# One ring of six PSUM banks for the front stage of a hybrid encoder layer

## The chip, the cores and the metric

The kernel runs on one core of a Trainium2 chip. The metric is the device time of one execution in microseconds (us); the kernel before takes 859.18 us, the median of three runs between 858.85 and 859.22. The engines are named as in the profile: PE (TensorE, matrix products), DVE (VectorE), ACT (ScalarE), POOL (GpSimd) and SP (SyncE, which only issues transfers here). PE writes its results into PSUM, which has eight banks; one bank holds a tile of 128 partitions by 512 numbers in fp32. A bank can be used again when the engines that read the result (DVE and ACT) are through with it.

## The reference

One layer of an encoder for a prompt and a sample, each of 256 tokens with 1024 features (512 tokens in all). From the normalised input one wide projection is made, cut into parts for three branches:

```
h = rmsnorm(x);  proj = h @ w_in          # 9952 columns
A: q,k,v = silu(conv5(...)); gated delta rule forward and backward, in chunks   (8 heads)
B: latent attention: q and k,v from low-rank latents, rotary key; softmax        (8 heads)
C: cross-attention into 256 memory tokens                                        (4 heads)
merged = sum over branches of sigmoid(gate) * ((branch * silu(z)) @ w_br)
y = rmsnorm(x + merged @ w_out) * final_gain
```

All is in fp32. Products whose precision matters are made from split operands, as described below.

## The kernel before, in words

**Products.** Features stand on the partitions and the 512 tokens along a row. `gemm` (L234) makes one tile of 128 output features by 512 tokens. Each operand is split into a rounded part `hi` (ACT, L210) and a rest `lo` (DVE, L214), and three products are summed (hi·hi, lo·hi, hi·lo), so a tile with 1024 input features takes 24 matmuls. `weight` (L199) loads a weight tile into one of two raw buffers and splits it into one of two `wh` and one of two `wl` buffers. `gemm_fm` is the same as `gemm`, done at once.

**Stages.** `run` (L1310) has a front (`front`, L1390), a middle and a back. The front makes the memory values (`mem_v`, L356), the memory keys, the four memory heads (`mem_attn`, L470), the latents, the decays, and two groups of four latent-attention heads (`mla_rope`, `mla_v`, `mla_qk`, `mla_attn`). Between these steps `fills` (L1374) takes products from a list: tiles of q, k and v for the delta rule (`qkv_tile`), merge gates (`gate_tile`) and others. From the first latent head on, the preparation of the delta rule (`gdn_prep`, L777) is drawn along in small pieces at a low priority. The middle runs the delta rule beside the rest of the fill list; there the order on PE is written out by hand (`weave`). The back makes the last branch and the output.

**One attention step** (`attend`, L298), for one head and one of the two sequences: score products into a bank `s_` (L308); maximum (DVE), exponentials with row sums (ACT, L322), scaling by the reciprocal sum (`p_`, L328 or L330); four transposes on PE into a bank `pt_` (L334), which are the turned probabilities; their split into `ph` (ACT) and `pl` (DVE) at L222 and L224; and six products with the values into a bank `oa` or `om` (L343), which one head keeps for both sequences. At the end of a latent head DVE multiplies this output into the gate `za` (L727); at the end of a memory head ACT copies it out (L486).

**PSUM before.** The front has a pool of eight banks under four tags; `self.banks` is 3:

- `gm`, three banks: all products of `gemm`, the fourth value tile (`vm3`, `v3`), some small sums
- `kk`, two banks: scores, the two rope products `ra` and `rb`, row sums (`ss_`) and broadcasts
- `ms0`, two banks: turned probabilities, value tiles 0 and 2, and of the delta-rule preparation `dp` of the forward direction (L807, two matmuls with a sum) and `kd` (L815, 128 small matmuls, read by DVE at L828, L856 and L858)
- `ms1`, one bank: attention outputs, value tile 1, `dp` of the backward direction

The middle and the back have a pool of their own over the same banks, with `self.banks` at 4: four `gm`, which also serve `kk`, two `ms0`, two `ms1`.

**What sets the order.** In the front the order of every engine's instructions is made by a planner of the framework when the kernel is built. It goes by the order in the source, shifted by the stated `high_priority` offsets (a latent head's attention stands 50 instructions earlier, weight splits 60, weight loads 1000, the preparation 300 later), and issues on each engine the first instruction that its model of the times takes to be ready. A tile counts as ready to be written when a bank of its tag is free in that model. On the chip each engine then runs its instructions in that fixed order, and waits where a result or a bank is late. The weights' transfers are issued on SP's queue, the copies to DRAM on ACT's and SP's. `issue_after` puts instructions behind a named one on the same engine. In the middle, PE's order is fixed by `weave` and doesn't depend on the planner.

Of the kernel before, what the change touches and what calls it, by code (L numbers as in the profile page):

```python
# [7 lines left out]
F32 = mybir.dt.float32  # L8
# [5 lines left out]
P = 128  # L14
# [142 lines left out]
class Layer:  # L157
# [9 lines left out]
        return self.ps.tile([P, 512], F32, tag="gm", bufs=self.banks, name=name)  # L167

    def ps_kk(self, name):
        if self.banks == 4:  # L170
            return self.ps_gm(name)
        return self.ps.tile([P, 512], F32, tag="kk", bufs=2, name=name)

    def ps_ms(self, par, name):
        return self.ps.tile([P, 512], F32, tag=f"ms{par}", bufs=1 if par and self.banks == 3 else 2, name=name)

    def big(self, i, name, dt=F32R):

# [177 lines left out]
    def mem_v(self):  # L356
        nc, A = self.nc, self.A
        ms = []
        warm = self.p0.tile([P, 1], F32, name="warm")
        nc.vector.memset(warm, 0.0)  # L360
        nc.scalar.activation(warm, warm, AF.Square)

        zero = self.s2("zero", F32R)
        nc.vector.memset(zero.bitcast(F32), 0.0)
        zp = self.ps_kk("zp")
        for i in range(10):
            nc.tensor.matmul(zp, zero[:, 0:P], zero, start=i == 0, stop=i == 9)

        vps = [self.ps_gm(f"vm{tb}") if tb == 3 else self.ps_ms(tb % 2, f"vm{tb}") for tb in range(4)]
        acc = self.s2("mem2")  # L370
        raws = []
        with self.tc.high_priority(offset=1000):
            for k in range(8):
                if k % 2 == 0:
                    pair = self.big(k // 2, f"memT{k}", F32)
                raw = pair[:, k % 2]
                wr = self.pa.tile([P, 512], F32, tag="V", bufs=8, name=f"wr_vm{k}")
                nc.sync.dma_start(raw, A["memT"][:, k])
                d = (nc.sync if k else nc.scalar).dma_start(
                    wr, A["wvm"][k // 2][:, (k % 2) * 512:(k % 2 + 1) * 512])  # L380
                if k == 0:
                    nc.sync.dma_start(self.prm, A["prm"])
                raws.append((raw, wr))
        self.after = d.ins
        for k, (raw, wr) in enumerate(raws):
            hl = self.pk.tile([P, 2, 512], F32R, tag="kq", bufs=8, name=f"mh{k}")
            hi = self.p0.tile([P, 1024], F32R, tag="wh", bufs=2, name=f"wh_vm{k}")
            lo = self.p0.tile([P, 1024], F32R, tag="wl", bufs=2, name=f"wl_vm{k}")
            if k:
                nc.scalar.activation(hi[:, :512], wr, AF.Copy)  # L390
            else:
                nc.vector.tensor_scalar(hi[:, :512], wr, 1.0, None, ALU.mult)
            rnd = self.split(raw, hl[:, 0], hl[:, 1], self.mg[:, k:k + 1])
            nc.vector.tensor_tensor(lo[:, :512], wr, hi[:, :512].bitcast(F32), op=ALU.subtract)
            ms.append((hl[:, 0], hl[:, 1]))
            for i, (a, b) in enumerate(((0, hi), (1, hi), (0, lo))):
                for tb in range(4):
                    t = slice(tb * P, (tb + 1) * P)
                    nc.tensor.matmul(vps[tb], ms[k][a][:, t], b[:, :512],  # L399
                                     start=k == 0 and i == 0, stop=k == 7 and i == 2)  # L400
            with self.tc.issue_after(rnd.ins) if k == 0 else nullcontext():
                self.add_square(acc, raw, k, 1)
        self.mem_xs = ms
        self.cst = self.p0.tile([P, _CST.shape[1]], F32, name="cst")
        nc.sync.dma_start(self.cst, A["cst"])
        rm = self.rms_cols(acc, "mem")
        self.vm = []
        for tb in range(4):
            hi = self.pa.tile([P, 512], F32R, tag="V", bufs=8, name=f"vmh{tb}")
            lo = self.pa.tile([P, 512], F32R, tag="V", bufs=8, name=f"vml{tb}")  # L410
            self.split(vps[tb], hi, lo, rm[:, tb:tb + 1])
            self.vm.append((hi, lo))
        self.rm = rm
# [261 lines left out]
    def mla_v(self, g):  # L675

        nc, A = self.nc, self.A
        hi, lo = self.weight(A["wv"][g], 1024, f"wv{g}")
        vt = self.vt = []
        for tb in range(4):  # L680
            if tb == 2:
                self.fills(1)
            t = slice(tb * P, (tb + 1) * P)
            ps = self.ps_gm(f"v{g}{tb}") if tb == 3 else self.ps_ms(tb % 2, f"v{g}{tb}")
            n = 0
            for a, j in ((hi, 0), (hi, 1), (lo, 0)):
                for k in range(2):
                    nc.tensor.matmul(ps, self.kl[k][j][:, t], a[:, k * 512:(k + 1) * 512],
                                     start=n == 0, stop=n == 5)
                    n += 1  # L690
            vh = self.pa.tile([P, 512], F32R, tag="V", bufs=8, name=f"vh{g}{tb}")
            vl = self.pa.tile([P, 512], F32R, tag="V", bufs=8, name=f"vl{g}{tb}")
            self.split(ps, vh, vl)
            vt.append((vh, vl))
# [615 lines left out]
    def run(self):  # L1310
        nc = self.nc
        with ExitStack() as st:

            stp = ExitStack()
            self.ps, self.banks = self.pool(stp, "ps", bass.MemoryType.PSUM, reuse_waits="tile"), 3
            dp = self.pool(st, "dr", bass.MemoryType.DRAM)
            self.d_v = dp.tile([8, 512, P], F32, name="d_v")
            self.d_r = dp.tile([2, 32, 2, 384], F32, name="d_r")
            self.d_om = dp.tile([P, 4, 512], F32, name="d_om")
            self.d_z = dp.tile([P, 8, 512], F32, name="d_z")  # L1320
            self.d_xm = dp.tile([P, 4, 512], F32, name="d_xm")
            self.d_xa = dp.tile([P, 8, 512], F32, name="d_xa")
            self.d_n = dp.tile([8, 512], F32, name="d_n")
            self.d_m = dp.tile([8, P, 512], F32, name="d_m")
            self.d_g = dp.tile([2, 8, P, 512], F32, name="d_g")
            self.plan()
            self.p0 = self.pool(st, "p0")
            sth, stx = ExitStack(), st.enter_context(ExitStack())
            self.sth, self.stx = sth, stx
            self.ph = self.pool(sth, "ph", side="right")  # L1330
            self.setup()
            self.pk = self.pool(st, "pk")
            self.pb = self.pool(st, "pb")
            with ExitStack() as st2:
                self.pa = self.pool(st2, "pa")
                self.front()
            stp.close()
            self.ps, self.banks = self.pool(st, "pq", bass.MemoryType.PSUM, reuse_waits="tile"), 4
            with ExitStack() as st2:
                self.pg = self.pool(st2, "pg")  # L1340
                self.middle()
            with ExitStack() as st2:
                self.pe = self.pool(st2, "pe")
                self.back()
# [270 lines left out]
```

## Time and profile before

| | before |
|---|---|
| median of three runs | 859.18 us |
| the profiled execution | 859.05 us |
| its span, first to last instruction | 857.3 us |
| instructions | 13230 |
| PE busy | 845.6 us (99%), 4822 matmuls |
| DVE busy | 573.4 us (67%) |
| ACT busy | 451.9 us (53%) |
| POOL busy | 145.4 us (17%) |
| granted PE clock, mean | 0.999 |
| front / middle / back, by PE's products | to 369 us / 369 to 761 us / from 761 us |

A row of the timeline has the start in us from the span's start, the duration, the engine, the line of the kernel, the operation, the tiles it writes and reads, the shapes, and how many like it were merged; in brackets stands how long the engine was idle before it and what ended that. Matmuls overlap in the pipeline, so their durations are longer than the time that each adds; the spacing of their starts is what counts. A row in the list of waits has the engine and what it was about to do, what it waited for, the total in us, how often, and the longest. A row of the table of windows has, for PE, PEld (weight loads), DVE, ACT and POOL, the busy time and the count, then the granted clock, the share of the transfer engines and GB/s.

### The profile page before, as it was taken

To read this page: it belongs to the slowest core of one execution; us is meant where nothing else is said; L and a number is where in the kernel's file an instruction comes from. 1 tells how busy PE (TensorE), PEld (TensorE's weight loads), DVE (VectorE), ACT (ScalarE), POOL (GpSimd) and SP (SyncE) were. 2 spreads that over 40 slices of the span, in tenths; PEclk is the share of its full clock that TensorE was granted. 3 is DMA by queue.
4 is the path that set the end of the run, shared out by engine and by line. 5 is a ranking of instruction groups with operands and counts; after the bars stand their busy time and mean duration, and the time that the engine had idled before them with its cause. 6 is when DMAs were issued, how large, how long until landed. Compare 5 with 4: busy or idle time off the path is not lost.

```text
span 857.3 us, 13230 instructions
## 1 busy us (share of the span) xinstructions
PE 845.6 (99%) x4822; PEld 698.4 (81%) x4822; DVE 573.4 (67%) x1021; ACT 451.9 (53%) x891; POOL 145.4 (17%) x135
## 2 busy tenths in 40 slices
PE   9999999999999999999999999999999999999997
PEld 7878888888888888878788888888888888888886
DVE  7776347687599998457689998684555544346543
ACT  7655455455474465546775748666663632223232
POOL 0200111000100002072101254213110002332121
PEclk9999999999999999999999999999999999999999
DMA  9422222442425525363334365546445447375332
GB/s 326 141 79 87 86 81 68 139 138 75 103 77 164 137 90 146 116 191 129 109 103 122 117 189 174 152 134 180 132 122 160 138 134 250 118 241 160 116 98 99
DMA packets 68273, 116.10 MB, mean 135 GB/s; under 512 B 24048, under 2 KB 31600, under 8 KB 68208
## 3 DMA queue, kind: packets, MB, share of 16 engines
q1 hardware_dynamic: 46560, 104.51, 38.6%
q10 hardware_dynamic: 21648, 10.75, 4.6%
q8 instruction: 38, 0.62, 0.3%
q14 instruction: 27, 0.22, 0.1%
HBM read 95.09 MB, written 16.99 MB: 131 GB/s over the span
## 4 chain that ended last, share of the span: by engine, by line
PE 95%; DVE 2%; ACT 1%; issue 1%; DMA 1%; POOL 0%; POOLq 0%; ACTq 0%; DVEq 0%; SPq 0%
PE gm_qkv L246 16%; PE gm_g L246 16%; PE gm_z L246 8%; PE gm_bm L246 5%; PE gm_bg L246 5%; PE gm_za L246 5%; PE y L1256 5%; PE vm L399 3%; PE gm_be L246 3%; PE gm_qm L246 3%; PE gm_km L246 3%; PE kk L971 3%; PE o L1121 2%; PE gm_qn L246 2%; PE gm_cq L246 2%; PE s_a L308 2%
## 5 line engine op out<-in xcount | busy, mean ns | idle before, releaser
L745 DVE SCALAR_TENSOR_TENSOR kq<-cz,prm,kq 128x510 f32<-128x510 f32 (+1 forms) x64 | 48.1, 752 | 6.0 <-ACT kq L738 5.0
L246 PE MATMUL gm_qkv<-hh,wh_qkv 128*128 128x512 f32 x192 | 51.1, 400 | 0.5 <-ACT wh_qkv L210 0.5
L246 PE MATMUL gm_g<-hl,wh_g 128*128 128x512 f32 x192 | 51.5, 399 | 0.0
L246 PE MATMUL gm_g<-hh,wl_g 128*128 128x512 f32 x192 | 51.3, 398 | 0.0
L246 PE MATMUL gm_g<-hh,wh_g 128*128 128x512 f32 x192 | 51.1, 401 | 0.1
L246 PE MATMUL gm_qkv<-hh,wl_qkv 128*128 128x512 f32 x192 | 50.3, 397 | 0.0
L246 PE MATMUL gm_qkv<-hl,wh_qkv 128*128 128x512 f32 x192 | 49.7, 396 | 0.0
L214 DVE TENSOR_TENSOR wl_qkv<-wr_qkv,wh_qkv 128x1024 fp32r<-128x1024 f32 x24 | 31.1, 1297 | 25.9 <-ACT wh_qkv L210 10.1
L214 DVE TENSOR_TENSOR wl_g<-wr_g,wh_g 128x1024 fp32r<-128x1024 f32 x24 | 30.1, 1254 | 22.0 <-PE gm_g L246 11.7
L246 PEld LDWEIGHTS gm_qkv<-hl,wh_qkv 128*128 128x128 f32 x192 | 35.8, 188 | 8.2
L246 PEld LDWEIGHTS gm_qkv<-hh,wh_qkv 128*128 128x128 f32 x192 | 35.3, 188 | 8.9 <-ACT wh_qkv L210 1.2
L246 PEld LDWEIGHTS gm_qkv<-hh,wl_qkv 128*128 128x128 f32 x192 | 35.5, 188 | 7.8
L246 PEld LDWEIGHTS gm_g<-hl,wh_g 128*128 128x128 f32 x192 | 35.4, 188 | 7.7
L246 PEld LDWEIGHTS gm_g<-hh,wl_g 128*128 128x128 f32 x192 | 35.3, 188 | 7.5
L246 PEld LDWEIGHTS gm_g<-hh,wh_g 128*128 128x128 f32 x192 | 35.1, 188 | 7.8 <-ACT wh_g L210 0.3
L210 ACT ACTIVATE wh_qkv<-wr_qkv 128x1024 fp32r<-128x1024 f32 x24 | 25.4, 1058 | 29.1 <-PE gm_qkv L246 8.6
L1256 PE MATMUL y<-wh_wo,mh 128*128 128x512 f32 (+1 forms) x144 | 39.9, 370 | 0.0
L210 ACT ACTIVATE wh_g<-wr_g 128x1024 fp32r<-128x1024 f32 x24 | 25.4, 1060 | 26.0 <-PE gm_g L246 11.6
L961 POOL TENSOR_TENSOR kl<-kq,kh 128x512 fp32r<-128x512 f32 x16 | 22.8, 1427 | 94.8 <-ACT kh L959 94.8
L1226 POOL TENSOR_TENSOR mg<-mg,lg 128x512 f32<-128x512 f32 x16 | 27.2, 1700 | 59.0 <-DVE lg L1225 59.0
L246 PE MATMUL gm_bm<-xa,wh_bm 128*128 128x512 f32 x128 | 33.5, 398 | 0.0
L246 PE MATMUL gm_bg<-xg,wh_bg 128*128 128x512 f32 x128 | 32.5, 395 | 0.0
(432 smaller groups left out, 2199.5 us busy)
## 6 DMA issues: line engine op xcount, KB each, us to landing
wr_g<-in_w_dram SPq DMA_DIRECT2D x24, 512.0 KB
wr_qkv<-in_w_dram SPq DMA_DIRECT2D x24, 512.0 KB
e<-d_r SPq DMA_DIRECT2D x64, 96.0 KB
wr_z<-in_w_dram SPq DMA_DIRECT2D x12, 512.0 KB
d_g<-gt_g ACTq DMA_DIRECT2D x16, 256.0 KB
wr_za<-in_w_dram SPq DMA_DIRECT2D x8, 512.0 KB
wr_bm<-in_w_dram SPq DMA_DIRECT2D x8, 512.0 KB
lg<-d_g SPq DMA_DIRECT2D x16, 256.0 KB
```

Of the source, the lines that this page charges most:

```text
L210: self.wround = nc.scalar.activation(hi[:, :n], raw[:, :n], AF.Copy).ins
L214: d = eng.tensor_tensor(lo[:, :n], raw[:, :n], hi[:, :n].bitcast(F32), op=ALU.subtract)
L246: nc.tensor.matmul(ps[:m], a[:, k * m:(k + 1) * m], xs[k][j], start=n == 0, stop=n == 3 * nk - 1)
L308: nc.tensor.matmul(sp[:, qb * 256:(qb + 1) * 256], a, b, start=j == 0, stop=j == n - 1)
L399: nc.tensor.matmul(vps[tb], ms[k][a][:, t], b[:, :512], start=k == 0 and i == 0, stop=k == 7 and i == 2)
L745: nc.vector.scalar_tensor_tensor(ys, zs, self.cw[:, f, m:m + 1], ys, ALU.mult, ALU.add)
L961: nc.gpsimd.tensor_tensor(lo, src, hi.bitcast(F32), op=ALU.subtract)
L971: nc.tensor.matmul(ps, a[:, k], b, start=i == 0, stop=i == 2)
L1121: nc.tensor.matmul(out, ub[:, d, s, cp], rhs, start=n == 0, stop=n == 3)
L1226: nc.gpsimd.tensor_tensor(self.merged[d], self.merged[d], gt, op=ALU.add)
L1256: nc.tensor.matmul(ps, xs[2 * j + q][a][:, t], b[:, q * 512 + c0:q * 512 + c1], start=j == 0 and n == 0, stop=j == 3 and n == 5)
```

## The change

`self.banks` is 6 in the front: `gm` has six banks and serves products, scores, rope products, row sums and broadcasts, and whatever had `ms0` (turned probabilities, value tiles 0 and 2, `dp` forward, `kd`). `ms1` has two banks: attention outputs, value tiles 1 and 3, `dp` backward. So the shared part is six banks in place of 3 + 2 + 2, and the outputs have two in place of one. The pool of the middle and the back, with four banks in `gm` and two each in `ms0` and `ms1`, is as it was.

```diff
     def ps_gm(self, name):
         return self.ps.tile([P, 512], F32, tag="gm", bufs=self.banks, name=name)

     def ps_kk(self, name):
-        if self.banks == 4:
-            return self.ps_gm(name)
-        return self.ps.tile([P, 512], F32, tag="kk", bufs=2, name=name)
+        return self.ps_gm(name)

-    def ps_ms(self, par, name):
-        return self.ps.tile([P, 512], F32, tag=f"ms{par}", bufs=1 if par and self.banks == 3 else 2, name=name)
+    def ps_ms(self, par, name):
+        if self.banks == 6 and not par:
+            return self.ps_gm(name)
+        return self.ps.tile([P, 512], F32, tag=f"ms{par}", bufs=2, name=name)
...
-        vps = [self.ps_gm(f"vm{tb}") if tb == 3 else self.ps_ms(tb % 2, f"vm{tb}") for tb in range(4)]
+        vps = [self.ps_ms(tb % 2, f"vm{tb}") for tb in range(4)]
...
-            ps = self.ps_gm(f"v{g}{tb}") if tb == 3 else self.ps_ms(tb % 2, f"v{g}{tb}")
+            ps = self.ps_ms(tb % 2, f"v{g}{tb}")
...
-            self.ps, self.banks = self.pool(stp, "ps", bass.MemoryType.PSUM, reuse_waits="tile"), 3
+            self.ps, self.banks = self.pool(stp, "ps", bass.MemoryType.PSUM, reuse_waits="tile"), 6
```

## The prediction

> **What bounds the kernel now.** I read the page's shares and slices first, then a table of windows, then the list of what TensorE (PE) waited for, and last the timeline around each of those waits.
>
> ```profile
> PE 845.6 (99%) x4822; PEld 698.4 (81%) x4822; DVE 573.4 (67%) x1021; ACT 451.9 (53%) x891; POOL 145.4 (17%) x135
> ...
> PE   9999999999999999999999999999999999999997
> ...
> PEclk9999999999999999999999999999999999999999
> ```
>
> PE is busy from end to end at the full clock. A busy PE is not yet a PE at its peak, so the windows and the spacing come next: the two windows are the front from 120 us on and the middle.
>
> ```profile
> 120.00:369.00 249.00, 245.85 (x1377) 205.56 (x1377) 191.00 (x371) 136.73 (x271) 13.97 (x13) 1.00 0.38 113
> 369.00:760.00 391.00, 391.00 (x2484) 322.68 (x2483) 256.49 (x468) 214.97 (x456) 99.51 (x92) 1.00 0.48 148
> ```
>
> The middle has no idle PE at all; the front leaves 249.00 - 245.85 = 3.15 us. The chain of waits gives the spacing of matmuls that nothing holds up:
>
> ```profile
> 144.12 0.44 PE pt_m L334 x4
> ...
> 362.76 0.60 PE oa L343 x5
> ...
> 375.02 5.58 PE gm_g L246 x24
> ```
>
> So one matmul of 512 columns takes 5.58 / 24 = 0.2325 us of PE, one of 256 columns 0.60 / 5 = 0.12, one transpose 0.44 / 4 = 0.11. The amount of matmul work is the same after the change, so it can win only what lies between these spacings. PE's waits:
>
> ```profile
> PE oa L343 <- DVE za L727: 1.1, 1, 1.1
> ...
> PE pt_a L334 <- ACT p_a L328: 0.6, 1, 0.6
> PE gm_qkv L246 <- ACT wh_qkv L210: 0.5, 1, 0.5
> PE s_m L308 <- ACT p_m L322: 0.4, 1, 0.4
> PE oa L343 <- DVE pl_a L224: 0.4, 1, 0.4
> ```
>
> Each occurs once. The first and the fourth are waits for a PSUM bank; the second and the fifth wait for data; the third waits for a rounded weight.
>
> **The change part by part.** No instruction is added or removed. What changes is which bank a result may use, and through that the order in which the planner lays out all engines, their DMA issues included.
>
> *Scores from the ring of six.* A score tile had two banks, and this one waited until the exponentials (ACT) had read the bank before last:
>
> ```profile
> 135.68 0.28 PE L308 MATMUL s_m<-km,qml 128*128 128x256 f32 x1
> ...
> 135.79 0.47 ACT L322 ACTIVATE p_m<-s_m,nb_m 128x256 f32<-128x256 f32 x1
> ...
> 136.40 0.50 PE L308 MATMUL s_m<-km,qmh 128*128 128x256 f32 x2 [0.45 <-ACT p_m L322]
> ```
>
> The next matmul was due at 135.68 + 0.12 = 135.80 and came at 136.40: 0.60 us lost, removed by a free third bank. Nothing else is due there in its place.
>
> *Two banks for attention outputs.* `oa` had one bank, which the next head could not write before DVE had multiplied it into `za`:
>
> ```profile
> 251.90 0.60 PE L334 MATMUL pt_a<-cst,p_a 128*128 128x128 f32 x4
> ...
> 252.89 0.69 DVE L727 TENSOR_TENSOR za<-za,oa 128x512 f32<-128x512 f32 x1
> ...
> 253.63 0.39 PE L343 MATMUL oa<-ph_a,vh 128*128 128x256 f32 x1 [1.13 <-DVE za L727]
> ...
> 255.17 0.86 PE L246 MATMUL ra<-qlh,wh_ra 128*128 128x512 f32 x3
> ...
> 257.27 0.60 PE L334 MATMUL pt_a<-cst,p_a 128*128 128x128 f32 x4
> ...
> 257.94 1.24 PEld L246 LDWEIGHTS gm_g<-hh,wh_g 128*128 128x128 f32 x6 [0.31 <-ACT wh_g L210]
> ```
>
> Due at 251.90 + 0.44 = 252.34, come at 253.63: 1.29 us. The rope product `ra` is also given a bank of the six; it could stand only behind the scores' two banks before and came at 255.17. Earlier, it would cover this hole and free its rounded-weight buffer sooner for `wh_g`, for which PE waited at 257.94 (due at 257.27 + 0.44 = 257.71, so 0.23 us). These two go together: 1.52 us.
>
> *Turned probabilities and the sums (`dp`, `kd`) from the six.* This is where the order changes most.
>
> ```profile
> 216.14 0.40 PE L809 MATMUL dp<-dr00tb,bd 128*128 128x512 f32 x1
> ...
> 216.46 1.30 PE L823 MATMUL kd<-kq 128*32 128x32 f32 x128
> ...
> 219.34 0.91 ACT L328 ACTIVATE p_a<-p_a,rs_a 128x256 f32<-128x256 f32 x2 [0.75 <-DVE rs_a L325]
> ...
> 234.87 0.40 PE L809 MATMUL dp<-dr00ct,bd 128*128 128x512 f32 x1
> ...
> 240.46 0.60 PE L334 MATMUL pt_a<-cst,p_a 128*128 128x128 f32 x4
> ...
> 241.67 0.68 DVE L858 TENSOR_TENSOR nd<-nd,kd 128x512 f32<-128x512 f32 x1
> ```
>
> `dp` (half summed at 216.14, finished at 234.87) and `kd` (216.46, last read at 241.67) sat in both banks that turned probabilities may use. The probabilities were ready at 219.34 + 0.91 = 220.25 and were turned only at 240.46: attention stood still for 20 us. PE lost nothing meanwhile, since fill products covered it, but the backlog then ran in one bunch up to 257, and the hole at 252 lies in that bunch. From six banks the turn can follow at once; its own worth is nothing (cover: the fills) and its effect is in the 1.52. If attention goes first, the delta-rule preparation on DVE goes later. It has room, since its next reader on POOL waits for the front's last `oa` anyway, whose buffers it reuses:
>
> ```profile
> POOL t L893 <- PE oa L343: 27.1, 1, 27.1
> ```
>
> 27 us of delay would cost nothing there.
> The Trainium skill, in Perfetto Trace Analysis, section Optimization Strategy, says that the same gap repeated on the engine that should be saturated can mean too little SBUF or PSUM for the next tile; by that rule PSUM is not short here, because no PE gap repeats, and the sum would be 859.05 unchanged, while the rows above show a shortage that makes no gap where it lies.
>
> *Values (`vm`, `v`) two in the six, two in the output pair; row sums and broadcasts from the six.* Nothing: no such tile is in the list of waits. Without cover, as much as the scores' wait, 0.60 each way.
>
> *What stays.* The wait for a rounded weight:
>
> ```profile
> 170.72 0.63 PE L246 MATMUL gm_kn<-klh,wl_kn 128*128 128x512 f32 x2
> ...
> 171.86 2.12 PE L246 MATMUL gm_qkv<-hh,wh_qkv 128*128 128x512 f32 x8 [0.51 <-ACT wh_qkv L210]
> ```
>
> Due at 170.72 + 2 x 0.2325 = 171.19, come at 171.86: 0.67 us, no bank in it. And the drain of the last head, behind which the middle's PE order begins:
>
> ```profile
> 363.20 1.80 PE L246 MATMUL gm_za<-hh,wl_za 128*128 128x512 f32 x7
> ...
> 365.19 0.88 PE L334 MATMUL pt_a<-cst,p_a 128*128 128x128 f32 x4
> 366.62 0.55 PE L334 MATMUL pt_a<-cst,p_a 128*128 128x128 f32 x3 [0.55 <-ACT p_a L328]
> 367.11 0.38 PE L343 MATMUL oa<-ph_a,vh 128*128 128x256 f32 x1
> 367.86 0.38 PE L343 MATMUL oa<-pl_a,vh 128*128 128x256 f32 x1 [0.37 <-DVE pl_a L224]
> ...
> 369.28 1.09 PE L246 MATMUL gm_qkv<-hh,wh_qkv 128*128 128x512 f32 x4
> ```
>
> 366.62 - (365.19 + 0.44) = 0.99, then 0.16 before 367.11 and 0.63 before 367.86: 1.8 us, on ACT and DVE, not on banks. The middle's new pool lies on the same banks; before, its first product followed the last `oa` by 0.12, so it waited for none. At worst it waits for one reader, 0.7 (the DVE multiplication by `oa`).
>
> *What the new order brings in.* The trace of before cannot show it. Every PE wait is one that the planner did not foresee, and a new order has its own. Lower bound: it also rids itself of the rounded-weight wait and the drain, -0.67 - 1.8 = -2.5. Upper bound: three waits as dear as the dearest row, 3 x 1.29 = +3.9. I take one wait of the size of the `wh_qkv` row, +0.5, as that is the commonest size in the list.
>
> **Sum.** -0.60 - 1.52 + 0.5 = -1.6. From the profiled execution's 859.05 this is 857.4. The median shown is 859.18, 0.13 above; I leave that out.
>
> **The rivals.**
>
> *Waits only change place* (859.0). Attention is a chain through DVE and ACT, and in the window from 120 to 369 DVE is busy 191 of 249 us. Where a bank no longer holds a step, the DVE behind it may: the hole at 252.34 needs `pl`, which DVE also makes. For it: the two data waits in the list, 1.0 us. Against it: six `oa` matmuls of the waiting head and nine of `ra` could have gone at 252.34.
>
> *The drain and the weight wait go too* (854.9). 859.05 - 2.12 - 0.67 - 1.8 = 854.5, and 0.4 for a wait as small as the `pl_a` row. For it: scores of the last head no longer need the bank of the head before. Against it: the drain's own rows wait for ACT and DVE.
>
> *Slower: fills are spent too early* (862.6). With more banks to draw from, the planner runs products ahead, and the last heads of both groups of four (246 to 258, and 360 to 369) stand without products beside them. The price of a bare chain is in the drain: the last za matmuls before it start at 363.20, and from there to the first `oa` of that head, 367.11, and its second, 367.86, are 3.9 to 4.7 us. Two bare chains cost up to 2 x 4.7 = 9.4 in place of the 1.29 + 0.23 + 1.8 = 3.3 there now, +6.1; with a part of it covered as today, half to two thirds, +3.5. It decides as soon as the last product of a group of heads ends before the last scores begin. Against it: attention is traced with a priority 50 instructions earlier, and the products it needs come out in the same order as before.
>
> *Long tenants crowd the six* lies inside that rival's price: `dp` and `kd` hold two of the six for 20 to 25 us, and four remain where products and scores had five.
>
> *The clock falls.* The first products of the program show what a lower clock would cost:
>
> ```profile
> L367 PE MATMUL zp<-zero x10: 396/632/796, 1.5 to 5.4; 128*128 128x512 f32 x10
> ```
>
> Ten starts in 3.9 us are 0.43 each, 0.2 more than 0.2325; a stretch of twenty at that pace costs 4 us: 861.4 with the gains kept. For it stands nothing in the rows from 17 us on, whose clock is 1.00.
> The Trainium skill, in TensorE: Matmul & The Clock Gate, section A second HAM failure mode: psum-queue depth-cycling, tells of a kernel whose cycling through PSUM banks left PE idle so often for moments that its clock went up and down; here the granted clock was 0.999 with the smaller rings, and no run yet shows the larger one.
>
> *The change does nothing* is part of the first rival: the planner would lay out the same order, which the 20 us stand-still makes unlikely.
>
> **How the numbers follow.** Forecast 857.4, chance 0.42, own range 856.4 to 858.4. Waits change place 0.23. Drain and weight wait go too 0.15. Fills spent too early 0.18. Clock 0.02. A measurement of this kernel tells about 0.2% from no change, 1.7 us: faster is under 857.46, slower over 860.9. The forecast's own spread lies across the lower bound; I count 0.27 of its 0.42 as faster. Faster: 0.27 + 0.15 = 0.42. Same: 0.15 + 0.23 and a little of the slower case, 0.39. Slower: 0.17 + 0.02 = 0.19. The range leaves out the far half of the slower case and a third of the best: 855.0 to 861.6.
>
> **What would show it.** Right: no wait of `oa` for `za` and none of scores for `p_m` in the list; `pt_a` within about 5 us of its probabilities after 216 us; the first `oa` to the last in a narrower bunch before the group's end; the middle's first product 1 to 2 us earlier than 369.28, and everything behind it moved by the same. Wrong: new PE waits of together over 2 us in the front; a drain before the middle's first product over 3 us; a middle that is no longer full, or a clock under 0.99.

## The result and the profile after

The changed kernel takes 958.19 us (median of 4 runs, 956.5 to 959.14) against 859.16 before: 1.1149 times as long, interval 1.1136 to 1.1162. The forecast was 857.4, the range ended at 861.6. It is 99 us slower, and the profiled execution (958.18 us, span 956.4) is read below.

The page's shares and slices of the kernel after:

```profile
span 956.4 us, 13220 instructions
...
PE 885.7 (93%) x4822; PEld 723.0 (76%) x4822; DVE 578.7 (61%) x1021; ACT 454.1 (47%) x891; POOL 143.6 (15%) x135
...
PE   9988687899977899988899999999999999999997
...
PEclk9997787999989899989899999999999999999999
```

PE has the same 4822 matmuls and is idle for 7% in place of 1%. Both the holes and the lower clock lie in the first half of the slices. The table of windows, with columns for PE, PEld, DVE, ACT and POOL and then the granted clock, says where:

```profile
0.00:120.00 120.00, 101.96 (x441) 81.76 (x442) 69.93 (x111) 59.50 (x102) 9.48 (x12) 0.89 0.36 124
120.00:369.00 249.00, 215.40 (x1087) 174.73 (x1086) 155.50 (x309) 103.91 (x194) 11.62 (x9) 0.92 0.27 82
369.00:470.00 101.00, 88.37 (x413) 71.21 (x412) 49.34 (x81) 46.00 (x94) 11.59 (x13) 0.92 0.38 115
470.00:860.00 390.00, 390.00 (x2478) 321.85 (x2477) 256.08 (x467) 215.32 (x457) 89.85 (x84) 1.00 0.46 143
```

The middle is as full as before (390.00 of 390.00 at clock 1.00). The front is not, and it ends later:

```profile
467.21 0.41 PE L343 MATMUL oa<-ph_a,vl 128*128 128x256 f32 x1
467.43 1.05 PE L246 MATMUL gm_qkv<-hh,wh_qkv 128*128 128x512 f32 x2
```

The middle's first product starts at 467.43 in place of 369.28: 98.15 of the 99 us. PE's list of waits (total, times, longest):

```profile
PE pt_a L334 <- ACT p_a L328: 18.2, 14, 3.3
PE pt_m L334 <- DVE p_m L330: 15.1, 4, 6.9
PE oa L343 <- ACT ph_a L222: 6.3, 9, 0.9
PE oa L343 <- DVE pl_a L224: 5.6, 7, 1.7
PE ss_q L267 <- POOL cqs L260: 4.1, 1, 4.1
PE rp L598 <- DVE ga L593: 3.3, 2, 2.9
PE om L343 <- ACT ph_m L222: 2.7, 4, 0.7
PE ss_k L267 <- POOL cks L260: 2.6, 1, 2.6
```

No row here waits for a bank. PE waits for data: turned probabilities (`pt`) for the softmax, outputs (`oa`, `om`) for the split of the turned tile, the sums (`ss`, `rp`) for POOL and DVE. One memory head shows it in the timeline of PE:

```profile
112.56 0.41 PE L308 MATMUL s_m<-km,qml 128*128 128x256 f32 x1
115.67 0.48 PE L334 MATMUL pt_m<-cst,p_m 128*128 128x128 f32 x1 [2.69 <-DVE p_m L330]
...
118.75 0.58 PE L343 MATMUL om<-ph_m,vmh 128*128 128x256 f32 x1 [0.69 <-ACT ph_m L222]
...
120.71 0.41 PE L334 MATMUL pt_m<-cst,p_m 128*128 128x128 f32 x1
120.78 2.06 PE L246 MATMUL gm_qm<-hh,wh_qm 128*128 128x512 f32 x4
122.63 1.91 PE L246 MATMUL gm_qm<-hl,wh_qm 128*128 128x512 f32 x4
```

After the last score product of the head's first sequence PE does nothing until the probabilities are there, and then begins to turn them. The products of the next head (`gm_qm`) come only at 120.78, right behind the first transpose of the second sequence (120.71), though nothing that they read is missing: both parts of their weights were ready at 101.3. And they run slowly: four from 120.78 to 122.63 are 0.46 us each, against 0.2325 before.

To size the two losses I went through the starts of successive PE matmuls, from the first of `vm` to the last of `oa`. What a distance has above 0.232, 0.118 or 0.108 us (512, 256, 128 columns) is booked as a wait if PE was idle in between, as slow running if it was not idle and the distance is over half as long again. Some 2.5 us of the slow running are very short products that every kernel has, and drop out of a difference. The rest of the front is 353 to 355 us of work in these two kernels.

```
front, us       length   waits   slow running
before          362.75     4.5       4.4
after           460.9     74.4      32.1
```

So 69.9 us of the 98.15 are waits and 27.7 slow running; 0.5 is left over.

**Where the order comes from.** In both kernels the first writers of all tiles of one tag stand on PE strictly in the order in which the program creates them; tiles of different tags pass each other. Before, 70 of 146 tiles of the front begin on PE after one that was created later, always one of another tag; after, 18. PE's instructions as the planner laid them out, around the first memory head:

```
before: s_m00, s_m01, abp, gm_qm1 x24, gm_cq0 x16, pt_m00 x4, gm_cq x12, pt_m01 x4, ... om0
after:  abp, s_m00 x6, pt_m00 x1, s_m01 x6, pt_m00 x3, om0 x6, pt_m01 x1, gm_qm1 x16, pt_m01 x3
```

Before, 40 products lie between scores and turn, which cover the softmax. After, a turned tile and the products draw on one ring. A bank of that ring goes to tiles in order of creation, so the products of the next head, created later, can't begin before the first transpose, which waits for the softmax. Counted in instructions at full speed, PE had 3.6 to 33.8 us of other work between the scores and the first transpose of an attention step before; after, 0 to 2.3 us in 20 of the 24 steps. This I call theory A. Its rivals: B, too many tenants in too few banks; and C, the clock falling by itself, because more banks are cycled through.

### The profile page after: what moved, and what is told of

Same layout as the page of the kernel before. It is cut to its first block, busy times and chain, and to the rows that moved or that the text cites. A ratio compares the mean times of both kernels' runs of the same rounds, so it can differ in the third digit from the quotient of the medians.

```text
span 956.4 us, 13220 instructions
## 1 busy us (share of the span) xinstructions
PE 885.7 (93%) x4822; PEld 723.0 (76%) x4822; DVE 578.7 (61%) x1021; ACT 454.1 (47%) x891; POOL 143.6 (15%) x135
## 4 chain that ended last, share of the span: by engine, by line
PE 87%; ACT 5%; DVE 5%; issue 2%; POOL 1%; DMA 0%; ACTq 0%; POOLq 0%; DVEq 0%; SPq 0%
PE gm_qkv L246 14%; PE gm_g L246 14%; PE gm_z L246 7%; PE gm_bm L246 5%; PE gm_bg L246 5%; PE y L1256 4%; PE gm_za L246 4%; PE gm_qm L246 3%; PE vm L399 2%; PE gm_be L246 2%; PE gm_km L246 2%; PE kk L971 2%; PE o L1121 2%; PE s_a L308 2%; PE gm_cq L246 2%
## 5 line engine op out<-in xcount | busy, mean ns | idle before, releaser
L246 PE MATMUL gm_qkv<-hh,wh_qkv 128*128 128x512 f32 x192 | 54.5, 422 | 0.0
L214 DVE TENSOR_TENSOR wl_g<-wr_g,wh_g 128x1024 fp32r<-128x1024 f32 x24 | 30.6, 1277 | 30.8 <-ACT wh_g L210 15.7
L246 PEld LDWEIGHTS gm_qkv<-hh,wh_qkv 128*128 128x128 f32 x192 | 38.2, 205 | 8.4
L214 DVE TENSOR_TENSOR wl_qkv<-wr_qkv,wh_qkv 128x1024 fp32r<-128x1024 f32 x24 | 31.0, 1294 | 16.6 <-ACT wh_qkv L210 8.1
L224 DVE TENSOR_TENSOR pl_a<-pt_a,ph_a 128x512 fp32r<-128x512 f32 x16 | 11.0, 687 | 42.4 <-ACT ph_a L222 42.1
```

The source lines that it names most:

```text
L214: d = eng.tensor_tensor(lo[:, :n], raw[:, :n], hi[:, :n].bitcast(F32), op=ALU.subtract)
L224: nc.vector.tensor_tensor(lo, src, hi.bitcast(F32), op=ALU.subtract)
L246: nc.tensor.matmul(ps[:m], a[:, k * m:(k + 1) * m], xs[k][j], start=n == 0, stop=n == 3 * nk - 1)
```

## The experiments

**One extra instruction (theory A against B).** The tile takes its bank with a product that needs no probabilities; the first transpose then overwrites it. The ring stays at six.

```diff
         tp = self.ps_ms(0, "pt_" + name)
+        nc.tensor.transpose(tp[:, 0:P], self.c("id"), self.c("id"))
```

> The kernel after with one transpose of the constant identity put ahead of the four transposes of each turned-probability tile: 24 short instructions more, written into the same bank and overwritten; ring, tags and source order as after. Theory A (banks of one tag are granted in source order, so a turned-probability tile that waits for its softmax holds back every product traced behind it): the tile's bank is claimed without waiting for the softmax, products go ahead, time 857 to 863 (before, plus 24 x 0.11 = 2.6, minus up to 2.1 of old waits), no PE wait of a transpose for p above 1.5 us in one piece except at the end of the front, granted clock 0.99 or more. Theory B (six banks are too few for all tenants): each bank is held through the softmax too, some 5 us longer, so at least as slow as after, 958 or more. Theory C (the clock falls because results cycle through more banks, and the waits follow from that): the same banks are cycled, clock at most 0.96, 945 or more.

881.17 us, 1.0253 of before (1.0237 to 1.0268), 18 us above the range given for theory A and far below those of B and C; front 384.95, waits 17.5, slow running 11.8. One more transpose per step takes back 77 of 99 us with the ring unchanged, so it is the place of the first writer that cost them. PE's waits in this kernel:

```profile
PE ss_q L267 <- POOL cqs L260: 4.1, 1, 4.1
PE rp L599 <- DVE ga L594: 2.9, 1, 2.9
PE ss_k L267 <- POOL cks L260: 2.6, 1, 2.6
PE rkb L282 <- POOL rk L640: 1.3, 1, 1.3
...
PE pt_a L335 <- ACT p_a L328: 0.5, 1, 0.5
```

`pt_m` is gone from the list, and `pt_a` fell from 18.2 to 0.5. What stays are the sums, the other tiles in the ring whose first product waits for a slow engine.

**Four banks in place of six.** `bufs=4` for the front's ring, two banks empty.

> The kernel after with four banks in the shared ring in place of six; two banks stand empty. Theory A: the order in which tiles begin is set by the source, not by the number of banks, so 955 to 970. Theory B: a third of the banks is gone, so the loss of 99 us grows by half or more, over 1000. Theory C: fewer banks are cycled, the clock and the time recover at least in part, under 930.

961.82 us, 1.1191 (1.1169 to 1.1214), 0.4% over the changed kernel; clock 0.953 as there (0.954). PE's first two waits:

```profile
PE pt_a L334 <- ACT p_a L328: 22.7, 13, 5.6
PE pt_m L334 <- DVE p_m L330: 15.2, 4, 6.9
```

Between four banks and six the number hardly matters in this order. That is against B, and against C.

**One half of the merge at a time.** From the kernel before, the ring of three takes in either the two banks of turned probabilities (with all that shares them) or the two of scores and sums, five in all.

```diff
 ms0_merged:
     def ps_ms(self, par, name):
+        if self.banks == 5 and not par:
+            return self.ps_gm(name)
...
 kk_merged:
     def ps_kk(self, name):
...
+        return self.ps_gm(name)
...
```

> The kernel before with one edit: turned probabilities, value tiles 0 and 2, dp forward and kd share a ring of five with the products; scores keep two banks and the outputs one. Theory A: where the turn follows the scores in the source with no product traced earlier that is still to run (the first three memory heads), products wait for the softmax; the latent heads' scores run ahead in their own banks and stay covered. The waits of after at those six turns come to some 15 to 20 us, and the clock falls there: 875 to 900. Theory B: five banks for the same tenants as before, 857 to 862. Theory C: no forecast between the two.

900.7 us, 1.048 (1.0459 to 1.0501), just above what was expected; front 404.6, waits 33.6, slow running 16.7. This half alone gives 41 of the 99 us; `pt_m` waits 9.8 us in three waits.

> The kernel before with the other edit alone: scores, rope products and sums share a ring of five with the products; turned probabilities keep two banks and the outputs one. Theory A: a score waits only for a split of q, which is short, so the ring is not held up: 856 to 861. Theory B: as before or a little better, 856 to 861. Theory C: more banks cycled, slower than 870.

875.03 us, 1.0182 (1.0165 to 1.0199), where theory A expected no loss and only C one of this size; front 378.5, waits 15.3, slow running 9.6. Its waits:

```profile
PE ss_q L265 <- POOL cqs L258: 4.1, 1, 4.1
PE rp L596 <- DVE ga L591: 2.9, 1, 2.9
PE ss_k L265 <- POOL cks L258: 2.6, 1, 2.6
PE rkb L280 <- POOL rk L637: 1.3, 1, 1.3
```

These are the rows that stayed in the first experiment. I had taken scores and sums to begin at once; scores do, sums don't. In the order on PE two products created after `ss_q` began ahead of it before, and two score tiles ahead of `rp`; with the rings merged none does. So the loss needs no C, and the source order below, with six banks, keeps the clock at 0.997.

The two halves give 41.3 + 15.7 = 57 us, the whole change 99. The order on PE tells where the rest is: 58 tiles of the front still pass an earlier one with the one half merged, 41 with the other, and 18 with both (70 before). With `ms0` merged only six of the 24 attention steps have under 3 us of other work between scores and turn, with `kk` merged none.

**All waiting tiles claimed.** The same claim for `ss`, `rkb`, `abp`, `gclp` and `rp` too, first with a small product, then with the 128-column transpose.

```diff
+    def claim(self, ps):
+        i = self.c("id")[0:32, 0:32]
+        self.nc.tensor.matmul(ps[0:32, 0:32], i, i, start=True, stop=True)
...
 claim_wide:
+        self.nc.tensor.transpose(ps[:, 0:P], self.c("id"), self.c("id"))
...
```

> The kernel after with a 32x32 product of the identity, written ahead of everything else into the bank of each turned-probability tile and of the five tiles of sums that wait for other engines (ss_q, ss_k, rkb, abp, gclp and rp); 30 short matmuls more, overwritten at once. Theory A (source order within a tag): what the run with claims for the turned probabilities alone still lost, 21.8 us over before, is the same thing at the sums (waits of 4.1, 2.6, 1.3, 2.9 and 0.7 us) and the clock that fell there (0.92 from 60 to 145 us), so 856 to 863, granted clock 0.995 or more. Theory B (too few banks): the sums hold their banks longer, 881 or more. Theory C (cycling through more banks lowers the clock): 875 or more, clock under 0.99.

872.99 us, 1.016 (1.0145 to 1.0175); waits 6.1, slow running 12.9. The waits went as expected, the time did not (856 to 863 was expected). Part of it is the claims: each is two instructions on PE and lengthens the distances of starts around it by about 0.37 us, 9.6 us over the 26 claims that have no wait beside them. The view of the turned tile has them:

```profile
L171 PE MATMUL pt_m<-cst x16: 191/202/212, 66.8 to 152.8; 32*32 32x32 f32 x16
```

> As the run with claims for all waiting tiles, but each claim is one 128x128 transpose of the identity in place of a 32x32 product, which was written as two instructions that each held PE for about 0.14 us more than nothing (9 us over 60). Thirty transposes of 0.11 to 0.15 us. Theory A: with nothing held back by source order the six banks are as good as the old ones, 859.3 + 30 x 0.14 = 863.5, so 860 to 865. If the remainder of the run before was not the claims' own cost, 870 or more.

870.53 us, 1.0124 (1.0108 to 1.0141): not the 860 to 865 expected if the claims' own cost were all that was left, but the other case, 870 or more. Front 373.2, of which the claims are 3.3 (0.11 each), waits 9.4, slow running 7.5. Cheaper claims won 2.5 us only, as the waits rose. Against before, 3.3 of claims, 4.9 of waits and 3.1 of slow running make up the 11.3 us of loss. In its list of waits:

```profile
PE gm_qm L249 <- ACT p_m L327: 1.4, 1, 1.4
PE gm_qkv L249 <- DVE qnl L227: 0.9, 1, 0.9
PE gm_qm L249 <- ACT sq L262: 0.9, 1, 0.9
```

These are products that wait for a reader to leave a bank: a tile that claims early also holds early. Here B has its part, about 4 us of waits (with two rows of 0.4). It shows only once A is out of the way.

**The source in another order, the six banks untouched.** Attention is split in two: scores and softmax, created first; then the products that were created behind it; then turn and output. The sums are created later in the same way.

```diff
...
+                with self.tc.high_priority(offset=50):
+                    p = self.mla_scores(4 * g + h, *cur)
                 if h < 3:
                     nxt = self.mla_qk(4 * g + h + 1, gate)
                 else:
                     gate()
                 with self.tc.high_priority(offset=50):
-                    self.mla_attn(4 * g + h, z[0], *cur)
+                    self.mla_turn(4 * g + h, z[0], p)
...
```

> The kernel after, six banks in one ring and no instruction added; only the source order differs: scores and softmax of a head are traced before the products that follow, their turn after them, and the sums a product later. Theory A: 856 to 863, clock 0.995 or more, no PE wait of a transpose for p over 1.5 us. Theory B: the same tenants in the same banks, held longer by the scores, 945 or more. Theory C: the same cycling, 945 or more.

863.34 us, 1.0048 (1.0033 to 1.0063), 0.3 above the range; front 366.9, waits 7.0, slow running 5.0, clock 0.997. The same tiles, banks and products: 95 of the 99 us hang on the order of creation. The costliest wait behind the first products:

```profile
PE oa L348 <- ACT ph_a L222: 1.5, 2, 1.1
```

**The same source order with the rings of before.** The two kernels differ in nothing but the rings.

> The source order of the run with the six banks (scores and softmax traced ahead of the following products, turn and sums after them), but with the rings of before (3, 2, 2 and 1). It tells what of that run's 863.3 belongs to the source order and what to the ring. Theory A: with separate rings the source order matters little, 857 to 862. If the reorder itself costs (more scores at once, two softmax results waiting longer), 862 to 866, the same as with the six banks.

856.49 us, 0.9967 (0.9954 to 0.998): faster than both kernels by a little, and half a us below the range expected. Its waits, all of them, and the middle's first product:

```profile
PE zp L372 <- DVE zero L369: 1.5, 1, 1.5
PE oa L348 <- DVE pl_a L224: 1.3, 1, 1.3
PE om L348 <- ACT ph_m L222: 0.3, 1, 0.3
```

```profile
366.74 1.56 PE L246 MATMUL gm_qkv<-hh,wh_qkv 128*128 128x512 f32 x6
```

366.74 is 2.54 us ahead of before. Waits of `oa` for `za`, of `s_m` for `p_m` and of `gm_qkv` for its weight, which the prediction priced, are all gone, with one output bank and two score banks. In a square:

```
median us               order of before    new order
rings of before              859.2           856.5
six and two                  958.2           863.3
```

The shared ring loses in both columns: 99.0 and 6.9 us.

**The second output bank alone.** From before: `ps_ms` always two banks, the products' ring two in place of three.

> The kernel before with one edit: two banks for attention outputs in place of one, paid for with a product bank (two in place of three); scores and turned probabilities keep their own two. It measures what the second output bank is worth by itself. Theory A and the prediction's step: the wait of oa for za (1.1 us) is gone, and two product banks are enough because a product's bank is given back within 1 to 2 us of its last matmul, 856 to 861. Theory B: a product bank less costs more than it brings, over 865.

865.94 us, 1.0073 (1.0056 to 1.009): not the 856 to 861 that the prediction's step stands for, but the other case, over 865. `oa` no longer waits for `za`, but two products wait for the split of the values to leave a bank:

```profile
PE gm_qkv L246 <- DVE vl L224: 2.7, 1, 2.7
PE gm_g L246 <- DVE vl L224: 2.4, 1, 2.4
```

In this split a third bank for products is worth more than a second for outputs. The values' tile that holds the bank is the fourth, which stayed in the products' ring here, while the change moved it to the outputs' pair; no run has the two apart.

**The stand-still of attention.** From before: `dp` forward and `kd` go to the scores' banks, away from the turned probabilities.

```diff
-            dp = self.ps_ms(d, f"dp{g}{d}")
+            dp = self.ps_ms(d, f"dp{g}{d}") if d or self.banks == 4 else self.ps_kk(f"dp{g}{d}")
...
-        kp, kqs = self.ps_ms(0, f"kd{g}"), [self.kq[h0 + h] for h in range(4)]
+        kp, kqs = self.ps_kk(f"kd{g}") if self.banks == 3 else self.ps_ms(0, f"kd{g}"), [self.kq[h0 + h] for h in range(4)]
```

> The kernel before with dp forward and kd in the scores' two banks in place of the two of turned probabilities. It is the prediction's step on the 20 us stand-still alone: attention is turned some 10 us of PE work after its scores in place of 34. The prediction's step holds if the 1.1 us wait of oa for za and the bunch before it go away: 856.5 to 858.5. If the stand-still has nothing to do with that wait, 858.5 to 861.

861.22 us, 1.0026 (1.0015 to 1.0036), 0.2 above the range for no connection. The work on PE between scores and turn of that head falls from 34 to 13 us, and nothing is won. The wait of `oa` for `za` falls from 1.1 to 0.4 us, that of `pt_a` rises from 0.6 to 1.7, and small new ones come in:

```profile
PE pt_a L334 <- ACT p_a L328: 1.7, 2, 1.1
PE rb L246 <- ACT p_a L322: 0.5, 1, 0.5
PE oa L343 <- DVE za L727: 0.4, 1, 0.4
```

**The clock as a cause.** The changed kernel with a ring of five and, in the sixth bank, eight products of no use (on data long there) behind the scores of each step, 192 in all, 44.6 us.

```diff
...
+        fp = self.ps.tile([P, 512], F32, tag="fl", bufs=1, name="fl_" + name)
+        with self.tc.issue_after(last):
+            for i in range(FILL):
+                nc.tensor.matmul(fp, self.h[0][0][:, 0:P], self.h[0][0], start=i == 0, stop=i == FILL - 1)
```

> The kernel after with five banks in the shared ring and eight filler products (512 columns, result unused) behind the scores of each attention step in a bank of their own, so that PE works while the softmax runs; 192 matmuls more, 44.6 us of PE at full clock, of which the waits for p (33 us in after) and ph, pl (15) take up the most. It tells the share of the clock in the 99 us from that of the waits. If the half-speed matmuls seen in after (202 in the front, about 0.15 us too long each) cost some 25 to 30 us by themselves: clock 0.98 or more and 930 to 950. If the clock costs nothing beside the waits: 956 to 975.

955.91 us, 1.1126 (1.1104 to 1.1148), at the edge of the range for a clock that costs nothing beside the waits (956 to 975), and above that for one that does. With 44.6 us more work it is no slower than the changed kernel. Waits fell to 42.5 us and slow running to 16.6, both by about half; the clock rose from 0.954 to 0.981. Slow running goes with the waits. It was not separated from them further: no run has the waits at full clock. That more banks alone do not lower the clock is shown by the new source order, 0.997 with six.

## Why the prediction was wrong

The reading of before held. Three changes to the trace that the prediction named as signs of being right came: no wait of `oa` for `za`, none of scores for `p_m`, turned probabilities at once behind their softmax. They came with 99 us of loss, so they were no proof of a gain. The fourth sign didn't come: the middle's first product was to start 1 to 2 us earlier and started 98 us later. Two of the signs of being wrong came with it, new waits of 69.9 us in place of at most 2, and a clock of 0.954, under 0.99; the middle stayed full.

**The step that failed** is the one on turned probabilities and sums from the six: "From six banks the turn can follow at once; its own worth is nothing (cover: the fills)". The turn did follow at once. But the fills named as its cover share its ring now and are created behind it, so they can't begin before it. The cover was gone, and the bare chain through DVE and ACT stood on PE's path: 33.3 us in the two `pt` rows and 14.9 in those of `oa` and `om` (6.3 + 5.6 and 2.7 + 0.3), 2.0 us for each of the 24 attention steps. I had read `dp` and `kd` holding the turn back for 20 us as a shortage; the experiment on the stand-still says that it cost nothing; in the rows of before, products ran through it. To be late was harmless; to be bound to it was not.

**Row sums and broadcasts**, put at "Nothing" and bounded at 0.60 either way, failed for the same reason. That a tile is in no list of waits tells that its cover holds, not that it can do without. Merged alone, scores and sums cost 15.7 us.

**"What the new order brings in"**, +0.5 with bounds of -2.5 and +3.9, was the term of the sum that should have held this. Its upper bound was three waits as dear as the dearest in the list. Those rows come from an order in which products may pass; a bound had to come from what lies between scores and turn in the rows of before. The prediction had such a price, 3.9 to 4.7 us for a bare chain from the drain, and counted two chains where the front has 24 attention steps. As a loss the price was read too high: in the 3.9 us from 363.20 to 367.11 PE also ran eight products and eight transposes, 8 x 0.2325 + 8 x 0.11 = 2.7 us of work. That 24 times the price, 94 to 113 us, lies about the 98 that were lost is chance, as those 98 hold the waits for sums and the slow running too.

**Scores and outputs** (-0.60 and -1.52): the waits did go, but they were no reason to share. With the new order and the rings of before they are gone too, and in the six banks the same order is 6.9 us slower. A second output bank alone lost 6.7 us, as it was paid for with one of the products.

**The rivals.** "Fills are spent too early" had the sign and the price of a bare chain, but the fills came too late. "Waits only change place" and "Long tenants crowd the six" can be seen once the order is mended, in the 4 us of new waits of the claims and perhaps in the 6.9. "The clock falls" was given 0.02 on the ground of a larger ring; the clock did fall, to 0.954, but four banks give the same (0.953), and it goes with the waits. Of the trigger that the Trainium skill tells of in TensorE: Matmul & The Clock Gate, section A second HAM failure mode: psum-queue depth-cycling, the runs bear out that short idle moments of PE go with a lower clock (69.9 us of new waits, 0.954 in place of 0.999); the number of banks had no part in it.

The Trainium skill's rule in Perfetto Trace Analysis, section Optimization Strategy, that the same gap repeated on the engine that should be saturated can mean too little SBUF or PSUM for the next tile, would point at banks in the profile after, where `pt_a` waits 14 times. With four banks in place of six the time is 961.82 against 958.19; the gap repeats because of the order in which banks are granted, and the measurement decides against that reading here.

**Left open:** that the two halves of the merge add up to 57 us and not 99 fits the order on PE, where each half leaves other work free to pass; how many us that is worth was not measured. Of the 6.9 us that the six banks lose in the new order, 5 are waits (7.0 against 2.0 us by the count of starts), among them those of `oa` and `om` for the splits and of a score for its split `q`; slow running is the same within half a us. No run divides them further. What the slow running would be without the waits, or the waits without it, stays open too.

## What to carry to other kernels

A ring of buffers is also an order: where banks go to tiles as they are created, a tile whose first writer waits for another engine holds up every tile created behind it, whether the ring has four banks or six. Before pooling, write down for each tenant what its first writer waits for and what covers that wait; tenants that begin at once and tenants that wait need rings of their own, or a source order in which each stands where it can begin. A step that has no row in the list of waits may owe that to the very work which the change ties to it.

## What the runs showed of the hardware

PE ran slowly behind waits of under 3 us. In the kernel with two output banks (and two for products) a single wait stood ahead of it:

```profile
174.47 2.72 PE L246 MATMUL gm_qkv<-hh,wh_qkv 128*128 128x512 f32 x8 [2.73 <-DVE vl L224]
176.99 3.01 PE L246 MATMUL gm_qkv<-hl,wh_qkv 128*128 128x512 f32 x8
```

The eight matmuls from 174.47 took 0.315 us each on average and the eight from 176.99 to 179.83 took 0.355, against 0.2325, behind a wait of 2.73 us; the granted clock was 0.72 from 174 to 180 us and 1.00 in the next 10. With waits as dense as in the changed kernel, the clock stayed low for tens of microseconds:

```profile
60.00:90.00 30.00, 21.55 (x91) 16.55 (x90) 13.49 (x24) 9.89 (x21) 0.00 (x0) 0.77 0.12 36
90.00:120.00 30.00, 22.41 (x97) 18.21 (x96) 9.58 (x19) 10.04 (x19) 3.56 (x3) 0.79 0.24 79
```

In the kernel before, the clock is 1.00 in both stretches. Over the whole front 69.9 us of waits came with 27.7 of slow running, 1.4 us lost for each us of waiting; that the one brings the other is not shown. And a 32 x 32 product in f32 is not free: it stands as two instructions, together about 0.37 us of PE for each claim, where a 128-column transpose took 0.11.
